# Two hybrid decoder layers on one core: new prices and a new limit in the estimate that orders the mixing stage

## The chip, the cores and the metric
The kernel runs on one core of a Trainium2 chip. The metric is the time of one execution on the device in microseconds (us). TensorE does the matrix products (PE in the profile), VectorE (DVE), ScalarE (ACT) and GpSimd (POOL) the rest, and SyncE (SP) starts the DMA transfers.

## What is computed
Input and output are 512 tokens of 1024 channels in float32. Two layers of the same form follow each other:

```python
for l in range(DEPTH):                       # DEPTH = 2
    x = _layernorm(ALPHA * x + 0.5 * _swiglu(x, ffn1_w_in[l], ffn1_w_out[l]), ...)
    mix = _hybrid_mixer(x, l, mix_w_in[l], ...)
    x = _layernorm(ALPHA * x + mix, ...)
    x = _layernorm(ALPHA * x + 0.5 * _swiglu(x, ffn2_w_in[l], ffn2_w_out[l]), ...)

def _hybrid_mixer(x, ...):
    h = x @ w_in                             # one projection for everything below
    ya = _rwkv7(h[..., 0:o1], ...)           # 8 heads of 64: decay, delta rule, group norm
    yb = _diff_attention(h[..., o1:o2], ...) # 4 heads: two softmaxes, one minus lam times the other
    yc = _gated_deltanet(h[..., o2:o3], ...) # 4 heads: causal conv, chunks of 64, gated delta rule
    branches = jnp.einsum('blnc,ncd->blnd', stack([ya, yb, yc]), w_branch)
    gates = sigmoid(h[..., o3:])
    return (gates * branches summed over the three) @ w_out
```

## The kernel before, in words
**Products.** The stream is held transposed as two parts of float32r, a high part `xTh` and a low part `xTl`; a weight tile `wr` comes by DMA, ScalarE casts its high part `wh`, VectorE subtracts to get the low part `wl`, and a product is made of three matmuls, high by high, low by high and high by low, each 128x512. A column of the projection is 8 tiles of 128 channels, so 24 such matmuls (`proj`, tile name `pj`; `pz` and `pgt` are the same for other columns). They depend on nothing but the weights and the stream, so TensorE can do them at any time: they are what fills it between the mixers' small products.

**The mixing stage.** It has 12 units, in the order `R D R D R R D G G D G G` (`ORDER`), numbered from 0 within their kind: R is a pair of RWKV heads (`rw_pair`), D a head of differential attention (`da_head`), G a head of the gated delta rule (`gdn_head`). For each unit the projection columns are made first (3 or 4), then the unit's mixer starts as a generator that does one step, yields, does the next. `gdn_ab` and its chain of small VectorE operations (tiles `gq`, `gg`, then the products `pG`) come after R0. At the end `merge` multiplies the three branches by their gates; for each branch it first has every open mixer of that kind run out (`finish`).

**What sets the order.** Everything is issued in the order in which the Python program calls it, and a framework's scheduler may then move instructions a little on each engine. `interleave` alternates: one step of the main generator (a few products), then as many steps of open mixers as `pump` gives, until the estimated time of TensorE has grown by `CAP` = 1300 ns. `Estimate` (L81 to L131) keeps that time: `log` adds to each engine's clock the price of an instruction (`c_pe`, `c_act`, two lambdas), and notes when each tile will be ready. A mixer's next step is taken when the estimated end of its last step (`it[2]`) is no later than TensorE's estimated clock (`self.est.pe.t`). A price that is too low makes a step look ready too early, so that it is issued with too little other work ahead of it.

**The limit on open units.** Before a new unit may have its columns made, `unit` (L1334) calls `pump(True)` while four mixers are open. A forced pump takes the mixer whose last step ends first by the estimate, ready or not. The tiles of the mixers come from one pool of 53 buffers of 128x512 (`T2B`).

**Names used below.** R unit: `pM` are the chunk products that VectorE masks into `M`; `pMV`, `paT` are turned into `R` by VectorE; `pW` is the product of the solved triangle `iZ` by `R`; then a scan of four steps `pU`, `VU`, `pS`, `S`; `Y` is the group-normed result, `pyT<-Y` its transposes, `pgl` its gate. D unit: `pdo` the attention's output, `dO` its scaling by the norm (`norm_T`), `pyT<-dO` its transposes. G unit: `pk`, `gL`, `gr` the decays, `iZ`, `ip` the solving of the triangle, `pv`, `vn`, `po`, `gO` the scan, `pyT<-gO` the transposes; `cv`, `ct` the convolution in `gdn_conv`. `rst`, `rsy` are the tiny operations of a reciprocal square root on VectorE (`rsqrt`), `Tb` and `LX` those that solve a triangle by rows.

Of the kernel before, what the change touches and what calls it, by code (L numbers as in the profile page):

```python
# [13 lines left out]
ALU = mybir.AluOpType  # L14
# [29 lines left out]
AHEAD = 2  # L44
LOADED = 1
BLK = 8 * (16 * 128 + 16)
WIDTH = 4
CAP = 1300.0
PJB = 3
T2B = 53  # L50
# [4 lines left out]
class Queue:  # L55


    def __init__(self, eng, cost, est):
        self.eng, self.cost, self.est, self.t = eng, cost, est, 0.0
        self.last, self.inorder = None, False  # L60
# [20 lines left out]
class Estimate:  # L81
# [3 lines left out]
    def __init__(self, tc):  # L85
        nc = tc.nc
        self.tc = tc
        q = lambda eng, cost: Queue(eng, cost, self)
        self.nc, self.ready, self.stage = nc, {}, 0.0
        self.tensor = q(nc.tensor, self.c_pe)  # L90
        self.vector = q(nc.vector, lambda op, n, k: 70 + n * (0.52 if op in ("tensor_scalar", "tensor_copy") else 1.04))
        self.scalar = q(nc.scalar, self.c_act)
        self.gpsimd = q(nc.gpsimd, lambda op, n, k: 600 + 150 * n if k.get("op") == ALU.pow else 150 + 2.1 * n)
        self.sync = q(nc.sync, None)
        self.pe = self.tensor
        self.queues = (self.tensor, self.vector, self.scalar, self.gpsimd)
# [8 lines left out]
    def c_pe(self, op, n, k):  # L105
        m = k["out"].shape[0]
        if op == "transpose":
            return 107
        if k["rhs"].dtype == F32R:
            return n / 2.4 / (1 if m > 32 else 4)  # L110
        return max(107, n / 0.6) / (1 if m > 64 else 1.7 if m > 32 else 2.7)

    def c_act(self, op, n, k):
        return 80 + n / 1.2 + (94 if any(hasattr(k.get(x), "tensor") for x in ("scale", "bias")) else 0)

    def log(self, q, op, args, kw):
        names = ("out", "lhsT", "rhs") if op == "matmul" else ("out", "in_", "identity")
# [17 lines left out]
class Net:  # L135
# [1196 lines left out]


    def unit(self, n, h):  # L1334
        while sum(it[0] < 3 for it in self.active) >= WIDTH:
            self.pump(True)
        cols = (h, 4 + h, 8 + h)
        if n == 0:
            mixer, cols = self.rw_pair, [self.rw_col(c) for c in cols]
        elif n == 1:  # L1340
            mixer, cols = self.da_head, [self.da_col(c) for c in cols]
        else:
            mixer, cols = self.gdn_head, [self.gdn_conv(c) for c in (4 + h, h, 8 + h)] + [self.gdn_z()]
        f = []
        for g in cols:
            f.append((yield from g))
            yield
        self.active.append([n, mixer(h, *f), self.est.stage])
# [73 lines left out]
```

## Time and profile before

| what | value |
|---|---|
| median of 3 runs | 2872.88 us (2869.75 to 2876.25) |
| the profiled execution's own time | 2870.58 us |
| its span, first to last instruction | 2868.8 us |
| mean granted clock of TensorE | 0.998 |
| PE busy | 2819.2 us, 98% of the span |
| DVE busy | 1651.9 us, 58% |
| ACT, POOL busy | 1009.7 us, 158.3 us |
| mixing stage of the first layer | about 400 to 900 us of the span |
| mixing stage of the second layer | about 1827 to 2327 us |

In the timeline views a row has start, duration, engine, line, operation, output and inputs, shape and count, and in brackets the idle time just before it on its engine with what ended it. Matmuls overlap in the records (one of 128x512 is listed at 0.39 us and the next begins about 0.23 us later), so idle time below some 0.16 us before a matmul is not seen. Almost every instruction is put down to one line (L66), the recording helper; tiles' names tell them apart.

### The profile page before, as it was taken

How to read it: one execution, taken by the hardware profiler on the slowest of the kernel's cores; microseconds unless marked ns; L12 is line 12 of the kernel's file. 1: busy time of each engine (PE TensorE's matmuls, PEld its weight loads, DVE VectorE, ACT ScalarE, POOL GpSimd, SP SyncE). 2: the span in 40 equal slices, each digit the busy share in tenths (PEclk: the TensorE clock that was granted, in tenths of full speed). 3: DMA queues.
4: the chain of work that ended last, by engine and by line, in shares of the span. 5: the costliest groups of instructions: out<-in, count | busy, mean ns of one | idle time of the engine just before them, and what ended most of it. 6: DMA issues, size and time to landing. Idle time of an engine off the chain costs nothing. (4 is left out here: it accounts for less than half of the span.)

```text
span 2868.8 us, 40154 instructions
## 1 busy us (share of the span) xinstructions
PE 2819.2 (98%) x15728; PEld 2331.8 (81%) x15728; DVE 1651.9 (58%) x3752; ACT 1009.7 (35%) x1797; POOL 158.3 (6%) x204
## 2 busy tenths in 40 slices
PE   9999999999999999999999999999999999999998
PEld 8888887778888888888888888777788888888887
DVE  4333567788874463433643445677888755633345
ACT  3222345444543332222322223454545433322222
POOL 1000021110000010000100000211100000100001
PEclk9999999999999999999999999999999999999999
DMA  6433423222232353333424334232221334533332
GB/s 179 127 100 97 142 78 81 70 62 61 61 83 82 96 177 103 104 101 97 147 89 126 96 96 139 84 81 58 69 61 53 86 86 116 163 109 97 96 96 88
DMA packets 436349, 282.17 MB, mean 98 GB/s; under 512 B 39432, under 2 KB 391872, under 8 KB 436160
## 3 DMA queue, kind: packets, MB, share of 16 engines
q1 hardware_dynamic: 436160, 279.60, 33.4%
q8 instruction: 124, 2.03, 0.3%
q14 instruction: 65, 0.53, 0.1%
HBM read 258.31 MB, written 21.25 MB: 97 GB/s over the span
## 5 line engine op out<-in xcount | busy, mean ns | idle before, releaser
L66 DVE TENSOR_TENSOR wl<-wr,wh 128x1024 fp32r<-128x1024 f32 x406 | 502.1, 1237 | 648.9 <-ACT wh L66 647.8
L66 ACT CAST wh<-wr 128x1024 fp32r<-128x1024 f32 x406 | 427.5, 1053 | 1229.8 <-issue 535.8
L66 PE MATMUL pu<-xTh,wh 128*128 128x512 f32 x672 | 261.6, 389 | 0.0
L66 PE MATMUL pu<-xTl,wh 128*128 128x512 f32 x672 | 261.5, 389 | 0.0
L66 PE MATMUL pu<-xTh,wl 128*128 128x512 f32 x672 | 261.4, 389 | 0.0
L66 PE MATMUL oa<-wh,hl 128*128 128x512 f32 x640 | 249.0, 389 | 0.0
L66 PE MATMUL pg<-xTl,wh 128*128 128x512 f32 x640 | 249.0, 389 | 0.0
L66 PE MATMUL oa<-wh,hh 128*128 128x512 f32 x640 | 249.0, 389 | 0.0
L66 PE MATMUL pg<-xTh,wh 128*128 128x512 f32 x640 | 249.0, 389 | 0.0
L66 PE MATMUL pg<-xTh,wl 128*128 128x512 f32 x640 | 249.0, 389 | 0.0
L66 PE MATMUL oa<-wl,hh 128*128 128x512 f32 x640 | 249.0, 389 | 0.0
L66 PE MATMUL pj<-xTh,wh 128*128 128x512 f32 x560 | 228.5, 408 | 1.5 <-DVE sh L66 1.5
L66 PE MATMUL pj<-xTl,wh 128*128 128x512 f32 x560 | 225.0, 402 | 0.0
L66 PE MATMUL pj<-xTh,wl 128*128 128x512 f32 x560 | 223.9, 400 | 0.0
L66 DVE TENSOR_TENSOR ft<-ft,pu 128x512 f32<-128x512 f32 x84 | 57.8, 688 | 226.9 <-PE pu L66 226.8
L66 PE MATMUL pgt<-xTh,wh 128*128 128x512 f32 x384 | 154.1, 401 | 0.0
L66 PE MATMUL pgt<-xTh,wl 128*128 128x512 f32 x384 | 150.5, 392 | 0.0
L66 PE MATMUL pgt<-xTl,wh 128*128 128x512 f32 x384 | 149.6, 390 | 0.0
L66 PEld LDWEIGHTS pu<-xTh,wh 128*128 128x128 f32 x672 | 126.3, 188 | 26.1
L66 PEld LDWEIGHTS pu<-xTh,wl 128*128 128x128 f32 x672 | 126.1, 188 | 26.1
L66 PEld LDWEIGHTS pu<-xTl,wh 128*128 128x128 f32 x672 | 126.2, 188 | 26.0
L66 PEld LDWEIGHTS pg<-xTl,wh 128*128 128x128 f32 x640 | 120.2, 188 | 25.1
(392 smaller groups left out, 5282.5 us busy)
## 6 DMA issues: line engine op xcount, KB each, us to landing
wr<-in_ffn_w_in_dram SPq DMA_DIRECT2D x176, 512.0 KB
wr<-in_mix_w_in_dram SPq DMA_DIRECT2D x132, 512.0 KB
wr<-in_ffn_w_out_dram SPq DMA_DIRECT2D x88, 512.0 KB
wr<-in_mix_w_branch_dram SPq DMA_DIRECT2D x24, 512.0 KB
xres<-x SPq DMA_DIRECT2D x40, 256.0 KB
x<-xres SPq DMA_DIRECT2D x40, 256.0 KB
wr<-in_mix_w_out_dram SPq DMA_DIRECT2D x16, 512.0 KB
iX<-Xd SPq DMA_DIRECT2D x24, 256.0 KB
```

Source lines behind the costliest of these rows:

```text
L66: r = f(*args, **kw)
```

## The change
The estimate gets other prices on all engines, and the limit on open units another measure. `WIDTH` becomes 17 and is held against a sum of `ROOM`, 5 for an open R unit, 4 for a D, 4 for a G, 0 for the scalars' entry, with the new unit's own room included. VectorE costs 145 + 1.06 ns per element for every operation (62 more where a scalar comes from a tile); before it was 70 + 0.52 for `tensor_scalar` and `tensor_copy` and 70 + 1.04 for the others. ScalarE's base goes from 80 to 165, with 190 more for a sum on the side; GpSimd's from 150 to 250; float32r matmuls get 13.3 ns more and lose the division for few rows; float32 matmuls go from n / 0.6 to n / 0.57.

```diff
-WIDTH = 4
+WIDTH = 17
+ROOM = (5, 4, 4, 0)
...
-        self.vector = q(nc.vector, lambda op, n, k: 70 + n * (0.52 if op in ("tensor_scalar", "tensor_copy") else 1.04))
+        self.vector = q(nc.vector, self.c_dve)
         self.scalar = q(nc.scalar, self.c_act)
-        self.gpsimd = q(nc.gpsimd, lambda op, n, k: 600 + 150 * n if k.get("op") == ALU.pow else 150 + 2.1 * n)
+        self.gpsimd = q(nc.gpsimd, lambda op, n, k: 600 + 150 * n if k.get("op") == ALU.pow else 250 + 2.1 * n)
...
         if k["rhs"].dtype == F32R:
-            return n / 2.4 / (1 if m > 32 else 4)
-        return max(107, n / 0.6) / (1 if m > 64 else 1.7 if m > 32 else 2.7)
+            return n / 2.4 + 13.3
+        return max(112, n / 0.57) / (1 if m > 64 else 1.7 if m > 32 else 2.7)
 
     def c_act(self, op, n, k):
-        return 80 + n / 1.2 + (94 if any(hasattr(k.get(x), "tensor") for x in ("scale", "bias")) else 0)
+        return 165 + n / 1.2 + (94 if any(hasattr(k.get(x), "tensor") for x in ("scale", "bias")) else 0) + \
+            (190 if k.get("accum_out") is not None else 0)
+
+    def c_dve(self, op, n, k):
+        return 145 + 1.06 * n + (62 if any(hasattr(k.get(x), "tensor") for x in ("scalar", "scalar1")) else 0)
...
     def unit(self, n, h):
-        while sum(it[0] < 3 for it in self.active) >= WIDTH:
+        while sum(ROOM[it[0]] for it in self.active) + ROOM[n] > WIDTH:
             self.pump(True)
```

The limit bites at other units. Before, `pump` was forced ahead of the columns of R2 (three times), R3 (32), G1, G2 and G3. With the room, it is forced ahead of D1 (R0, D0 and R1 are open, and 14 + 4 is over 17), R2, D2, G0 (R2, R3 and D2 are open, again 14 + 4; 40 times, until D2 has ended), G1 and G3.

No instruction is added or taken away: TensorE, VectorE and the others have the same ones, in the feed-forward stages in the same order; in the mixing stages of both layers they stand in another order, the same in both. Since one line is added near the top, the helper's line is L67 in the kernel after. Three places of the new order follow; a row has the operation, output and inputs, the output's shape and the count.

**The solve of R1, on TensorE.** Before, this stands where unit R1's triangle is solved (`pW` is the product that needs the solved triangle) while unit D0 and the pair R0 end:

```order
L66 MATMUL paT<-ident,AR 128x128
L66 MATMUL pyT<-ident,dO 128x128 x2
L66 MATMUL paT<-ident,AR 128x128 x2
L66 MATMUL pW<-iZ,R 64x128 x8
L66 MATMUL pU_4777<-R,iZ 64x64 x16
L66 MATMUL pyT<-ident,Y 128x128 x4
L66 MATMUL pgl<-gdh,gup 128x512
L66 MATMUL pgl<-gdl,gup 128x512
L66 MATMUL pgl<-gdh,gup 128x512
L66 MATMUL pS<-VU,KB 128x128
L66 MATMUL pU<-M,R 128x128
L66 MATMUL pj<-xTh,wh 128x512
```

In the change the same place on TensorE reads:

```order
L67 MATMUL pyT<-ident,Y 128x128 x4
L67 MATMUL pgl<-gdh,gup 128x512
L67 MATMUL pgl<-gdl,gup 128x512
L67 MATMUL pgl<-gdh,gup 128x512
L67 MATMUL paT<-ident,AR 128x128 x4
L67 MATMUL pj<-xTh,wl 128x512
L67 MATMUL pj<-xTh,wh 128x512
L67 MATMUL pj<-xTl,wh 128x512
L67 MATMUL pj<-xTh,wl 128x512
L67 MATMUL pj<-xTh,wh 128x512
L67 MATMUL pW<-iZ,R 64x128 x8
L67 MATMUL pU_4532<-R,iZ 64x64 x16
```

Before, no product of the projection stands between `paT` and the scan's second step; now five stand between `paT` and `pW`, and nine more follow before the scan's `pS`. The transposes of `dO` have gone elsewhere.

**The start of R3, on TensorE and VectorE.** This is where unit R3's `pM` products end, while R2's scan (`pU`, `pS`) and unit D2's norm (`dss`, `dO`) run. In the change TensorE has, after the last `pM`:

```order
L67 MATMUL pS<-VU,KB 128x128
L67 MATMUL pj<-xTl,wh 128x512
L67 MATMUL pj<-xTh,wl 128x512
L67 MATMUL pyT<-ident,dO 128x128
L67 MATMUL pU<-M,R 128x128
L67 MATMUL pyT<-ident,dO 128x128 x3
L67 MATMUL pMV<-VU,M 64x64 x16
L67 MATMUL pS<-VU,KB 128x128
L67 MATMUL pU<-S,R 128x128
L67 MATMUL paT<-ident,AR 128x128 x4
L67 MATMUL pW<-iZ,R 64x128 x8
L67 MATMUL pU_5862<-R,iZ 64x64 x16
```

and VectorE at the same place, from the third of R3's four masks `M<-pM`:

```order
L67 TENSOR_TENSOR M<-pM,m_372 128x384
L67 SCALAR_TENSOR_TENSOR rst<-rst,dss 128x4
L67 TENSOR_TENSOR M<-pM,m_372 128x384
L67 SCALAR_TENSOR_TENSOR rsy<-rst,rsy 128x4
L67 TENSOR_TENSOR M<-pS,M 128x128
L67 TENSOR_TENSOR rst<-rsy 128x4
L67 SCALAR_TENSOR_TENSOR M<-M,Ef,bd 128x128
L67 SCALAR_TENSOR_TENSOR rst<-rst,dss 128x4
L67 TENSOR_TENSOR wl<-wr,wh 128x1024
L67 SCALAR_TENSOR_TENSOR dss<-rst,rsy 128x4
L67 TENSOR_SCALAR dO<-dO,dss 128x128 x4
L67 TENSOR_TENSOR VU<-pU,R 64x128
```

Before, 17 products of the projection stood between R3's `paT` and `pW`; now two stand from the last `pM` to the end of the solve. `pU`, `pS`, `VU` and `S` in between are R2's scan.

**The end of G0's scan, on VectorE.** In the change VectorE has, from the last `vn` of the scan (it needs `pv`) on, with the convolution of the next unit's column (`cv`) and the solving of another unit's triangle (`Tb`, `LX`) between:

```order
L67 COPY vn<-pv 128x128
L67 TENSOR_TENSOR iZ<-iZ,ip 128x512
L67 STREAM_TRANSPOSE iX<-iZ 128x512
L67 TENSOR_TENSOR gO<-gO,po 128x128
L67 TENSOR_SCALAR iZ<-ip 32x4x32 x2
L67 SCALAR_TENSOR_TENSOR cv<-pj,pt,cv 128x511
L67 TENSOR_SCALAR gss<-gss 128x4
L67 TENSOR_TENSOR Tb<-LX 32x15
L67 SCALAR_TENSOR_TENSOR cv<-pj,pt,cv 128x510
L67 TENSOR_SCALAR rst<-gss 128x4
L67 TENSOR_TENSOR LX<-LX,Tb 32x15
L67 SCALAR_TENSOR_TENSOR cv<-pj,pt,cv 128x509
```

24 more instructions follow, 22 of them tiny, one `rv` and one `ct`, and then `gO<-gO,gss` x4, which `pyT<-gO` on TensorE needs. TensorE has from that `pv` to `pyT<-gO` six small products of 128x128 (`ip`, `po`), 20 of 32x32 and 14 of `pz`.

## Rows read from the trace of the kernel before

**Rows 1.** The page's totals for TensorE (busy time, share of the span, instructions) and the clock granted to it in 40 equal slices, in tenths.
```profile
PE 2819.2 (98%) x15728; PEld 2331.8 (81%) x15728; DVE 1651.9 (58%) x3752; ACT 1009.7 (35%) x1797; POOL 158.3 (6%) x204
PEclk9999999999999999999999999999999999999999
```

**Rows 2.** Stretches of the span: a feed-forward stretch, then the early and the late part of each layer's mixing stage. Columns: length, busy time (and count) of PE, PEld, DVE, ACT, POOL, granted clock, share of the DMA engines, GB/s.
```profile
100.00:200.00 100.00, 100.00 (x443) 82.84 (x442) 38.84 (x44) 25.84 (x31) 0.00 (x0) 1.00 0.33 99
400.00:574.00 174.00, 163.61 (x1233) 129.91 (x1232) 133.40 (x433) 87.01 (x180) 24.06 (x28) 0.99 0.30 76
574.00:900.00 326.00, 322.33 (x2319) 262.44 (x2318) 258.44 (x874) 149.56 (x366) 17.04 (x25) 1.00 0.25 67
1827.00:2001.00 174.00, 162.85 (x1235) 128.79 (x1234) 134.20 (x432) 86.81 (x179) 23.06 (x28) 1.00 0.30 76
2001.00:2327.00 326.00, 322.12 (x2319) 262.29 (x2318) 258.51 (x874) 149.57 (x366) 16.84 (x24) 1.00 0.25 67
```

**Rows 3.** What TensorE waited for from 400 to 574 us: total, times, longest. Only the larger rows that are not in the next group.
```profile
PE pG L66 <- DVE gg L66: 2.0, 1, 2.0
PE pyT L66 <- DVE dO L66: 1.8, 2, 1.3
PE ip L66 <- DVE iZ L66: 1.1, 2, 0.9
PE pb L66 <- DVE dmx L66: 1.1, 1, 1.1
```

**Rows 4.** TensorE in order of time, where R1's `pM` end and its triangle is solved.
```profile
549.90 0.32 PE L66 MATMUL pM<-AR,sh 64*64 64x128 f32 x1
...
550.73 1.16 PE L66 MATMUL pdo<-dv,dsc 128*128 128x128 f32 x8
...
555.48 0.33 PE L66 MATMUL pMV<-VU,M 64*64 64x64 f32 x4 [0.75 <-DVE M L66]
...
560.41 0.30 PE L66 MATMUL pyT<-ident,dO 128*128 128x128 f32 x1 [0.49 <-DVE dO L66]
...
562.87 1.09 PE L66 MATMUL pW<-iZ,R 128*64 128x128 f32 x16 [1.40 <-DVE Tb L66]
563.77 1.13 PE L66 MATMUL pU<-R,iZ 128*64 128x64 f32 x32
564.83 0.66 PE L66 MATMUL pyT<-ident,Y 128*128 128x128 f32 x4
...
566.67 0.49 PE L66 MATMUL pS<-VU,KB 128*128 128x128 f32 x2 [0.48 <-ACT VU L66]
567.60 0.49 PE L66 MATMUL pU<-M,R 128*128 128x128 f32 x2 [0.44 <-DVE M L66]
568.86 0.63 PE L66 MATMUL pj<-xTh,wh 128*128 128x512 f32 x1 [0.77 <-DVE sh L66]
```

**Rows 5.** VectorE at the same place, in order of time. Between the first and the last row of the tiny operations stand 21 others of their kind.
```profile
557.63 0.16 DVE L66 TENSOR_TENSOR rst<-rsy 128x8 f32<-128x8 f32 x1
...
559.32 0.14 DVE L66 SCALAR_TENSOR_TENSOR dss<-rst,rsy 128x4 f32<-128x4 f32 x1
559.40 0.67 DVE L66 TENSOR_TENSOR Y<-Y,gn 128x512 f32<-128x512 f32 x1
560.00 0.85 DVE L66 TENSOR_SCALAR dO<-dO,dss 128x128 f32<-128x128 f32 x4
560.78 0.21 DVE L66 TENSOR_TENSOR LX<-LX,Tb 64x64 f32<-64x64 f32 x1
560.92 1.20 DVE L66 TENSOR_TENSOR wl<-wr,wh 128x1024 fp32r<-128x1024 f32 x1
562.05 0.67 DVE L66 TENSOR_TENSOR R<-paT,nn 128x512 f32<-128x512 f32 x1
```

**Rows 6.** VectorE's groups from 400 to 900 us, shapes kept apart: count, then busy us and mean ns of one, then the idle time before.
```profile
L66 DVE SCALAR_TENSOR_TENSOR cv<-pj,pt,cv 128x511 f32<-128x511 f32 x12 | 8.9, 739 | 0.8 <-ACT cv L66 0.7
L66 DVE STREAM_TRANSPOSE iX<-iZ 128x512 f32<-128x512 f32 x12 | 8.4, 702 | 0.1
L66 DVE TENSOR_TENSOR M<-pM,m 128x384 f32<-128x384 f32 x16 | 8.2, 546 | 0.1
L66 DVE SCALAR_TENSOR_TENSOR ct<-ct,cv 128x512 f32<-128x512 f32 x12 | 8.2, 683 | 1.2 <-ACT ct L66 1.2
L66 DVE TENSOR_TENSOR VU<-pU,R 64x128 f32<-64x128 f32 x28 | 8.0, 285 | 7.0 <-PE pU L66 6.5
L66 DVE TENSOR_SCALAR iZ<-ip 32x128 f32<-32x128 f32 x24 | 6.8, 283 | 3.8 <-PE ip L66 3.2
L66 DVE SCALAR_TENSOR_TENSOR M<-M,Ef,bd 128x128 f32<-128x128 f32 x12 | 4.2, 352 | 0.1
L66 DVE TENSOR_SCALAR dO<-dO,dss 128x128 f32<-128x128 f32 x16 | 3.5, 278 | 0.0
L66 DVE TENSOR_TENSOR R<-pMV,nn 128x512 f32<-128x512 f32 x4 | 2.8, 689 | 1.3 <-PE pMV L66 1.2
L66 DVE TENSOR_SCALAR lw<-lw 128x512 f32<-128x512 f32 x4 | 1.7, 426 | 1.1 <-ACT lw L66 1.1
```

**Rows 7.** TensorE's granted clock right after that place, in the first layer and in the second; columns as in the second group.
```profile
568.00:572.00 4.00, 3.23 (x10) 2.56 (x10) 2.61 (x7) 0.00 (x0) 0.00 (x0) 0.63 0.45 131
1996.00:2000.00 4.00, 3.33 (x16) 2.54 (x16) 2.68 (x6) 0.00 (x0) 0.00 (x0) 1.00 0.45 131
```

## The prediction
> **What bounds the kernel now.** I read the totals first: TensorE is busy for 98% of the span, every other engine for 58% or less [rows 1]. So the end is set by TensorE's own work plus the time in which it stands, and a change that leaves the work alone can only move the standing time. Next I read the windows, to see where it stands. A feed-forward stretch has none (100.00 of 100, 443 matmuls, so 100 / 443 = 0.226 us from one 128x512 matmul to the next) [rows 2]. The mixing stage has 174 - 163.61 = 10.4 us in its early part and 326 - 322.33 = 3.7 in its late part, in the second layer 11.2 and 3.9: 29.1 us in the two layers [rows 2]. VectorE is at 133.4 of 174 = 77% in the early part, 79% in the late: loaded, not full [rows 2]. So TensorE stands at places where small products that need VectorE follow each other with no projection product between.
>
> Then the waits: in the early part `pG` waits 2.0 us for the end of a VectorE chain, `pyT` 1.3 and 0.5 for `dO`, `ip` 1.1, `pb` 1.1 [rows 3]. The timeline shows the rest in one place, the solve of R1: 0.75, 0.49, 1.40, 0.48, 0.44 and 0.77, together 4.33 us within 14 [rows 4]. VectorE's timeline says why: with two reciprocal roots and a triangle on it, 23 tiny operations take 1.7 us, then come `Y`, four `dO` and a weight split `wl` of 1.20 us before the `R` that `pW` needs [rows 5].
>
> **What is left alone.** The change adds and removes no instruction, so the busy time of TensorE stays at its 2819.2 us [rows 1], and so do the feed-forward stages. The new prices are never executed; they cost nothing themselves. Transfers: the order of weight tiles is that of the plan, and the matmuls waiting for none of them in these windows is how I take the DMA queue to be no part of it (0 us; the DMA engines are at 25 to 33% [rows 2]).
>
> **R1's solve: -4.0 us per layer.** In the new order five projection products stand between `paT` and `pW` (5 x 0.226 = 1.1 us) and nine before the first `pS` (2.0 us), and `dO` with its transposes is gone from there. The 1.40 of `pW` came from `Y`, `dO` and `wl` ahead of `R`; the products now ahead of `pW` and after it cover what is left. I keep 0.3 for a `pS` behind `VU` and take 4.33 - 0.3 = 4.0 off. Bounds: -2.5 (only the three long waits 1.40 + 0.49 + 0.77 go) to -4.33.
>
> **R3's start: +5.3 us per layer.** The dense place is not gone, it comes back here. After the last `pM` TensorE has one `pS` and two products before it needs `dO`: 0.25 + 0.45 = 0.7 us. VectorE has from the third mask on: two `M` (0.546 each), `M<-pS` (about a `VU`'s 0.285), a scaled `M` (0.352), `wl` (1.20), five tiny ones at some 0.08 [rows 5, 6] and then the first `dO`. Operations overlap by some 0.06 each in the timeline, so this is 1.03 + 0.23 + 0.29 + 1.13 + 0.4 = 3.1 us, plus one `dO` and the way to TensorE, 0.3. That alone is 3.4 - 0.7 = 2.7 of waiting; TensorE makes the sixteen products of a pair of masks in 0.4 us (four masks' worth lasts 550.73 - 549.90 = 0.8 [rows 4]) while VectorE takes 1.03 for a pair, so VectorE is about another 0.5 behind when the last `pM` ends. I take 3.2. Then three more chains have almost no cover: the next `dO`s 0.2; the scan's `pU` behind `VU`, `R<-pMV` (0.689), `S` and its scaling, against 1.2 us of `pyT`, `pMV` and `pS`, 1.1; `pW` behind another `VU` and `R<-paT` (0.67 [rows 5]), against `pU` and `paT`, 0.8. Sum 3.2 + 0.2 + 1.1 + 0.8 = 5.3. Before, 17 products (3.8 us) stood between `paT` and `pW` here and nothing of this showed. Bounds: 1.0 (VectorE runs ahead of TensorE here, and only `wl` shows) to 7.
>
> On the four `dO`: the timeline has 0.85 us for four, 278 ns as a mean of one [rows 5, 6]. [...]
>
> **The end of G0's scan: +2.5 us per layer.** From the last `vn` on VectorE has `vn` (like `dO`, 0.28), `iZ<-iZ,ip` (like `ct`, 0.68), the transpose (0.70), `gO` (0.28), two `iZ<-ip` (0.57), three `cv` (2.2), `ct` (0.68), `rv` (0.28), some 25 tiny ones (1.7 to 2.3 at the pace of [rows 5]) and the first `gO` again (0.28): 7.7 to 8.3, less overlap (12 x 0.06 = 0.7), 7.0 to 7.6 [rows 6]. TensorE has 14 products (3.2 us), six small ones (about 0.8, by the pace of the `pyT` rows, 0.66 for four) and 20 tiny ones (about 1.3: `pU` runs 32 instructions in 1.06 [rows 4]): 5.3. Difference 1.7 to 2.3, plus the way over two queues: 2.5. Bounds: 0 (VectorE is ahead of TensorE when `pv` comes, and the convolution already done) to 4.
>
> **pG: +0.6 us per layer.** The chain of small operations that ends in `gg` now shares VectorE with three `wl`, eight `L` and more; I put the 2.0 [rows 3] at 2.6. Bounds: 0 (all hidden) to 4, so -2.0 to +2.0.
>
> **The rest.** The other early waits (`ip`, `pb`, the first `dO`, 1.1 + 1.1 + 1.3 [rows 3]) I leave, between -1.5 and +1.5, because units D1 and R2 are held back by forced pumps there. The 3.7 us of small waits in the late part [rows 2] should shrink with the better prices of short VectorE and ScalarE operations (base 145 in place of 70): I take -1.0, between -2 and +1.
>
> **The clock: +0.8 us in all.** [...] It cost (1 - 0.63) x 4 = 1.5 us once. The place at R3 stands longer in both layers; I give it a fall and a half against one: +0.8, between -1.5 and +1.7.
>
> **Sum.** Per layer -4.0 + 5.3 + 2.5 + 0.6 - 1.0 = +3.4; twice, +6.8; with the clock +7.6. The profiled execution took 2870.6 us, so 2878.2; the median of the runs stands 2.3 above it, which gives 2880.5, and I say **2880**.
>
> **Rivals.** A measurement of this kernel tells about 0.2%, 5.7 us, from no change.
>
> 1. *The new dense places are covered* (faster). R1's waits go, the tiny operations of D2's norm are done before R3's masks, so R3 costs 1.0 and G0 nothing; late waits lose 2. Per layer -4.0 + 1.0 + 0.6 - 2.0 = -4.4, and the fall of the clock goes: -8.8 - 1.5 = -10.3, 2863. For it: prices of 145 ns and more are nearer to the rows (285 for 64x128 where the old price gives 70 + 1.04 x 128 = 203), and steps should be issued less early. Against it: the two products behind the last `pM`.
>
> 2. *The waits only change places* (no change). R3 3.0, G0 1.0: -4.0 + 3.0 + 1.0 + 0.6 - 1.0 = -0.4 per layer, 2872. For it: VectorE has the same load, and its 77 to 79% [rows 2] leaves about the same slack anywhere.
>
> 3. *Forced pumps starve TensorE* (much slower). With the room, D1, R2, D2 and G0 wait for a unit to end; where nothing else is open, products for filling are only those that the three buffers of `pj` allow. The price is half of the early part's idle time again, 5 us per layer on top of the forecast, and one more fall: 7.6 + 10 + 1.7 = 19.3, 2892. It decides if the early part's VectorE share goes above some 82% while TensorE's falls.
>
> That the change does nothing is excluded: the order differs from R0 on.
>
> **Chances.** The forecast 0.42, rival 1 0.28, rival 2 0.20, rival 3 0.10. The forecast's own range is 2874 to 2886, of which a small part lies within 0.2%: faster 0.28, same 0.24, slower 0.48. The range takes in rival 1 but for its lower half, and reaches to rival 3: 2861 to 2892.
>
> **What would show it.** Right: at R1's solve `pW` follows without idle time, and `pyT<-dO` after the `pM` of R3 has some 3 us before it, `pU` and `pW` after it about 1 each; `pyT<-gO` of G0 has 2 to 3. TensorE's busy time in the mixing stage stays, its idle time goes from 29 to about 36. Wrong: if the waits of [rows 4] are still there, or if R3's transposes find `dO` ready; if idle time in the late part grows, the prices made it worse where I expect them to help.

## The result and the profile after
The change takes **2914.85 us** (median of 4 runs, 2913.31 to 2916.58) against 2874.18 for the kernel before beside it: ratio **1.0148**, 95% interval 1.0133 to 1.0163. It is slower, as forecast, but by 41 us and not by 7; 2880 is far off and 2892, the end of the range, too low.

The profiled execution has a span of 2911.8 us, 43.0 longer. The page's totals and clock of the change, which answer to [rows 1]:

```profile
PE 2836.7 (97%) x15728; PEld 2346.5 (81%) x15728; DVE 1668.1 (57%) x3752; ACT 1010.7 (35%) x1797; POOL 170.4 (6%) x204
PEclk9999999999999999999999999999999999999999
```

TensorE is busy for 17.5 us more with the same 15728 instructions, and stands for 43.0 - 17.5 = 25.5 us more. The windows over the mixing stages of the change (the late part 22 us longer, the second layer 22 us later; columns as in [rows 2]):

```profile
400.00:574.00 174.00, 168.46 (x1290) 131.63 (x1289) 134.54 (x418) 85.96 (x178) 20.52 (x26) 0.99 0.28 72
574.00:922.00 348.00, 326.19 (x2243) 268.14 (x2242) 260.86 (x856) 147.23 (x353) 24.70 (x26) 0.95 0.25 66
1849.00:2023.00 174.00, 168.65 (x1292) 131.68 (x1291) 134.29 (x417) 85.85 (x177) 22.33 (x26) 0.99 0.28 72
2023.00:2371.00 348.00, 325.88 (x2250) 267.77 (x2249) 261.57 (x859) 147.69 (x355) 25.41 (x26) 0.96 0.25 66
```

The early part has become better: 174 - 168.46 = 5.5 us of standing, where [rows 2] had 10.4. The late part has 21.8 where there were 3.7. So the added standing is all in the later half, where VectorE's share has gone down, 75% after 79%. What TensorE waited for, over the whole run of the change (total, times, longest):

```profile
PE pj L67 <- DVE dk L67: 10.1, 2, 5.0
PE pk L67 <- POOL sh L67: 7.4, 2, 3.7
PE pG L67 <- DVE gg L67: 6.2, 2, 3.1
PE pyT L67 <- DVE dO L67: 5.8, 2, 2.9
PE pz L67 <- DVE rsy L67: 5.5, 2, 2.8
...
PE pd L67 <- DVE gr L67: 3.1, 4, 1.2
PE pk L67 <- DVE gL L67: 3.1, 2, 1.6
```

The first two were in no list of mine. The `pk` stands early in unit R3, well before its `pM`, and waits for GpSimd. Timelines of TensorE, GpSimd and VectorE there, in the change:

```profile
589.27 0.40 PE L67 MATMUL pj<-xTh,wl 128*128 128x512 f32 x1
593.37 1.12 PE L67 MATMUL pk<-ident,sh 128*128 128x128 f32 x4 [3.70 <-POOL sh L67]
...
586.03 2.50 POOL L67 TENSOR_TENSOR AR<-sh,lw 128x256 f32<-128x256 f32 x2
588.49 2.50 POOL L67 TENSOR_TENSOR imL<-L,lev 128x512 f32<-128x512 f32 x2
590.94 2.37 POOL L67 TENSOR_TENSOR sh<-sh,G 128x512 f32<-128x512 f32 x1
...
587.26 0.67 DVE L67 TENSOR_TENSOR y<-y,sh 128x512 f32<-128x512 f32 x1
587.86 0.74 DVE L67 TENSOR_TENSOR Tb<-LX 64x64 f32<-64x64 f32 x1
...
592.12 1.27 DVE L67 TENSOR_TENSOR LX<-LX,Tb 64x63 f32<-64x63 f32 x1
...
593.58 0.20 DVE L67 TENSOR_TENSOR Tb<-LX 64x60 f32<-64x60 f32 x1
```

R3's `sh` stands behind two products `imL` of another unit's triangle in GpSimd's queue, and takes 2.37 us itself, where each of the four in a layer took 1.27 to 1.29 before. VectorE's tiny operations are listed at 0.74 and 1.27 us there, at 0.20 as soon as GpSimd's products have ended (593.3 us). So a part of the 3.70 us is that the two engines slow each other (in e7 below a tiny operation of VectorE comes every 1.22 us in place of every 0.25). Then the projection itself waits, for the eviction of a column (timelines of TensorE, ScalarE and VectorE in the change):

```profile
607.00 0.39 PE L67 MATMUL pj<-xTh,wl 128*128 128x512 f32 x1
612.43 0.76 PE L67 MATMUL pj<-xTh,wh 128*128 128x512 f32 x1 [5.05 <-DVE dk L67]
...
607.20 1.04 ACT L67 CAST wh<-wr 128x1024 fp32r<-128x1024 f32 x1 [4.38 <-PE pj L67]
608.26 1.17 ACT L67 CAST dk<-pj 64x512 fp32r<-64x512 f32 x2
...
608.27 1.22 DVE L67 TENSOR_TENSOR wl<-wr,wh 128x1024 fp32r<-128x1024 f32 x1 [0.24 <-ACT wh L67]
609.52 0.68 DVE L67 TENSOR_TENSOR dk<-pj,dk 64x512 fp32r<-64x512 f32 x1
...
611.59 0.69 DVE L67 TENSOR_TENSOR dk<-pj,dk 64x512 fp32r<-64x512 f32 x1
```

This is a ring. TensorE's last product of a column frees a weight buffer at 607.2; ScalarE, which stood 4.38 us for it, casts `wh`; behind that cast in ScalarE's queue stand the casts of `dk` that empty an older column (D2's keys, whose last product ran some 27 us before the wait ended), and VectorE's share of `dk` follows them; and the next column needs the buffer of that older one, the third of three. No engine is overloaded; each waits for another. The `wl` on VectorE adds little: it ends at 609.49, and ScalarE's first two casts of `dk` end at 609.43. [rows 4] had a hint of it: its `pj` stood 0.77 us for `sh`, which is an eviction too.

The granted clock right after such waits (columns as in [rows 2]; [rows 7] had one such window in two layers):

```profile
596.00:600.00 4.00, 4.00 (x11) 3.08 (x11) 3.80 (x7) 0.59 (x1) 1.78 (x2) 0.53 0.41 116
612.00:616.00 4.00, 3.57 (x12) 2.61 (x12) 2.75 (x10) 2.62 (x6) 0.00 (x0) 0.50 0.40 114
664.00:668.00 4.00, 3.47 (x48) 3.50 (x48) 2.54 (x4) 0.65 (x2) 0.00 (x0) 0.57 0.01 4
796.00:800.00 4.00, 4.00 (x21) 4.00 (x21) 0.68 (x2) 1.20 (x3) 1.27 (x1) 0.50 0.71 197
```

Over the mixing stages of the change the windows of 4 us lie between 0.50 and 1.00, called the lower and the upper level here; at 0.50, products of 128x512 follow each other 0.43 us apart (five intervals from 597.12 to 599.25 us). In the first window TensorE is busy all the time and gets through 11 matmuls; at the pace of [rows 2] it would be 4 / 0.226 = 18. Over the mixing stages, in windows of 4 us, (1 - clock) x 4 adds up to 34 us in the change and to 1.7 before.

### The profile page after: what moved, and what is told of

It reads as the page before. It is cut to its first block, busy times and chain, and to the rows that moved or that the text cites. A ratio compares the mean times of both kernels' runs of the same rounds, so it can differ in the third digit from the quotient of the medians.

```text
span 2911.8 us, 40172 instructions
## 1 busy us (share of the span) xinstructions
PE 2836.7 (97%) x15728; PEld 2346.5 (81%) x15728; DVE 1668.1 (57%) x3752; ACT 1010.7 (35%) x1797; POOL 170.4 (6%) x204
## 5 line engine op out<-in xcount | busy, mean ns | idle before, releaser
L67 DVE TENSOR_TENSOR wl<-wr,wh 128x1024 fp32r<-128x1024 f32 x406 | 500.1, 1232 | 658.8 <-ACT wh L67 658.0
L67 ACT CAST wh<-wr 128x1024 fp32r<-128x1024 f32 x406 | 427.2, 1052 | 1230.9 <-issue 556.2
L67 PE MATMUL pu<-xTh,wh 128*128 128x512 f32 x672 | 261.6, 389 | 0.0
L67 PE MATMUL pu<-xTh,wl 128*128 128x512 f32 x672 | 261.4, 389 | 0.0
L67 PE MATMUL pu<-xTl,wh 128*128 128x512 f32 x672 | 261.4, 389 | 0.0
L67 PE MATMUL oa<-wh,hl 128*128 128x512 f32 x640 | 249.0, 389 | 0.0
L67 PE MATMUL pg<-xTh,wh 128*128 128x512 f32 x640 | 249.0, 389 | 0.0
L67 PE MATMUL pg<-xTl,wh 128*128 128x512 f32 x640 | 249.0, 389 | 0.0
L67 PE MATMUL pg<-xTh,wl 128*128 128x512 f32 x640 | 249.0, 389 | 0.0
L67 PE MATMUL oa<-wh,hh 128*128 128x512 f32 x640 | 249.0, 389 | 0.0
L67 PE MATMUL oa<-wl,hh 128*128 128x512 f32 x640 | 249.0, 389 | 0.0
L67 PE MATMUL pj<-xTh,wh 128*128 128x512 f32 x560 | 228.6, 408 | 11.2 <-DVE dk L67 10.1
L67 PE MATMUL pj<-xTl,wh 128*128 128x512 f32 x560 | 227.6, 406 | 0.0
L67 PE MATMUL pj<-xTh,wl 128*128 128x512 f32 x560 | 225.1, 402 | 0.0
L67 DVE TENSOR_TENSOR ft<-ft,pu 128x512 f32<-128x512 f32 x84 | 57.7, 687 | 227.5 <-PE pu L67 227.4
L67 PE MATMUL pgt<-xTh,wh 128*128 128x512 f32 x384 | 154.6, 403 | 0.0
L67 PE MATMUL pgt<-xTh,wl 128*128 128x512 f32 x384 | 150.4, 392 | 0.0
L67 PE MATMUL pgt<-xTl,wh 128*128 128x512 f32 x384 | 150.1, 391 | 0.0
L67 PEld LDWEIGHTS pu<-xTl,wh 128*128 128x128 f32 x672 | 126.2, 188 | 26.1
L67 PEld LDWEIGHTS pu<-xTh,wh 128*128 128x128 f32 x672 | 126.2, 188 | 26.1
L67 PEld LDWEIGHTS pu<-xTh,wl 128*128 128x128 f32 x672 | 126.0, 188 | 26.1
L67 PEld LDWEIGHTS pg<-xTh,wl 128*128 128x128 f32 x640 | 120.3, 188 | 24.9
```

Of the source, the lines that this page charges most:

```text
L67: r = f(*args, **kw)
```

## The experiments
All times are medians beside runs of the kernel before (2873 to 2874 us). Two theories stood at first: **L**, the new limit makes the loss; **P**, the new prices do.

**e1_prices: the new prices, the old limit.**
```diff
-WIDTH = 17
-ROOM = (5, 4, 4, 0)
+WIDTH = 4
-        while sum(ROOM[it[0]] for it in self.active) + ROOM[n] > WIDTH:
+        while sum(it[0] < 3 for it in self.active) >= WIDTH:
```


> The new prices with the old limit of four open units. Theory L (the limit: with 17 for R, D and G only three units fit beside an R, so pumps are forced ahead of D1, R2, D2 and G0 and TensorE runs small products without projection products between): the loss is gone, 2862 to 2880 us, no wait of 3 us or more at pk, pj or pz, and one or two falls of the clock. Theory P (the prices: steps are issued later, columns of the projection are spent early, and evictions and chains pile up on VectorE): the loss stays, 2900 to 2920 us, with the same waits pk <- sh of 3.7 and pj <- dk of 5.


Measured: 2855.83 us, ratio 0.9935 (0.9920 to 0.9951). The prices are a gain of 17 us, more than theory L asked for. It is the fastest kernel of the study.

**e2_room: the new limit, the old prices.**
```diff
-WIDTH = 4
+WIDTH = 17
+ROOM = (5, 4, 4, 0)
-        while sum(it[0] < 3 for it in self.active) >= WIDTH:
+        while sum(ROOM[it[0]] for it in self.active) + ROOM[n] > WIDTH:
```


> The new limit (17, room 5, 4, 4) with the old prices. Theory L: most of the loss is here, 2895 to 2920 us, with a wait of some 3 to 5 us ahead of the products of D2 or G0. Theory P: about the time of the kernel before, 2865 to 2882.


Measured: 2890.40, ratio 1.0056 (1.0041 to 1.0071). The sign is theory L's; the +17 us are below its range, and the wait of 3 to 5 us that it named isn't there (the longest in the first layer is 2.01, at a `pyT`). The parts don't add: -17 and +17 alone, +41 together; under the new prices the limit costs 2915 - 2856 = 59 us.

**e3_w18 and e4_w19: 18 or 19 in place of 17** (e4 with 19 in the last line).
```diff
-WIDTH = 17
+WIDTH = 18
```


> The change with 18 in place of 17: two R, a D and another D or G fit together, so the pumps ahead of D1 and G0 go; those ahead of R2 and D2 (19) stay. Theory L: about half of the 42 us is gone, 2885 to 2900. Theory P: within 6 us of the change, 2908 to 2920.


Measured: 2878.39, ratio 1.0015 (1.0006 to 1.0025).


> The change with 19 in place of 17: R, R, D and R fit too, so none of the pumps ahead of D1, R2, D2 and G0 need be forced for the fourth unit. Theory L: as the new prices with the old limit, 2862 to 2880. Theory P: within 6 us of the change, 2908 to 2920.


Measured: 2871.73, ratio 0.9994 (0.9984 to 1.0003). Theory P is out: with the new prices in place, the limit alone takes the loss away. 18 takes away 36 of the 41 us, better than expected; it lets a fourth unit open ahead of D1 and of G0. 19 still holds R3 back where the old limit doesn't, and takes 16 us more than e1.

**e5_pjb4: the change with a fourth buffer for the projection's columns** (the ring above).
```diff
-PJB = 3
+PJB = 4
```


> The change with four buffers in place of three for the projection's columns (and four in place of five for the other accumulators). In the change a column waits 5.05 us for the eviction dk of a column that ended 27 us before. Theory B (the buffer is what it waits for, because the evictions of D2's columns stand late in VectorE's queue): that wait goes in both layers with the fall of the clock behind it, about 2 x (5.05 + 2) = 14 us, so 2898 to 2906 us. Theory S (TensorE runs dry here whatever the buffers, the wait turns up at the next small product): within 4 us of the change, 2911 to 2919; slower if the small products miss the fifth buffer.


Measured: 2897.80, ratio 1.0090 (1.0073 to 1.0107): 17 us less than the change. The row of that `pj`:
```profile
608.36 0.50 PE L67 MATMUL pj<-xTh,wh 128*128 128x512 f32 x1 [1.18 <-DVE dk L67]
```
5.05 has become 1.18. Theory B holds for the wait: the buffer is what the column waited for. Of the 17 us, 2 x (5.05 - 1.18) = 7.7 are this wait; the order of the matmuls moves with the buffer too, and other waits with it (`pk` from 3.70 to 2.58). That leaves 24 us over the kernel before.

**e6_kap: the product `sh` of the R unit on VectorE, priced as on GpSimd.**
```diff
-        nc.gpsimd.tensor_tensor(out=kap, in0=k, in1=G, op=ALU.mult)
+        kw = dict(out=kap, in0=k, in1=G, op=ALU.mult)
+        i = nc.vector.eng.tensor_tensor(**kw)
+        self.est.log(nc.gpsimd, "tensor_tensor", (), kw)
+        nc.vector.order(i.ins)
```


> The change with the product of k and G (tile sh, 128x512) of the R unit on VectorE instead of GpSimd, the estimate still pricing it on GpSimd. In the change pk waits 3.70 us for it behind two imL on GpSimd. Theory G (GpSimd's queue is what pk waits for): 3.7 and part of a fall of the clock go in each layer, 8 to 12 us less, 2902 to 2908 us. Theory V (VectorE is the one that is late there, and has one operation of 0.68 more now): pk waits for VectorE instead, within 4 us of the change, 2911 to 2919.


Measured: 2911.21, ratio 1.0134 (1.0119 to 1.0149), 4 us less than the change, within the two intervals.
```profile
598.21 0.50 PE L67 MATMUL pj<-xTh,wh 128*128 128x512 f32 x1 [3.31 <-DVE dq L67]
...
610.74 0.77 PE L67 MATMUL pj<-xTh,wh 128*128 128x512 f32 x1 [5.19 <-DVE dk L67]
```
The wait of `pk` is gone and a `pj` waits 3.31 us for VectorE a few us later. So theory G is right on the wait and wrong on the time. The time is theory V's, but what waits is a column for its buffer (`dq` is D2's queries), not `pk`: the next thing is late.

**e7_micro: VectorE's chains alone and beside GpSimd.** The layers are left out; chains (`d...A` alone, `d...P` beside six GpSimd products of 128x512) in which each operation needs the one before:
```python
V.tensor_tensor(out=t[0:64, 0:63], in0=t[0:64, 0:63], in1=x1[0:64, 0:63], op=ALU.mult)   # tiny
V.tensor_tensor(out=t, in0=t, in1=x1, op=ALU.mult)                                       # big
V.tensor_tensor(out=t[:, 0:128], in0=pp[:, 0:128], in1=t[:, 0:128], op=ALU.mult)         # psum: pp in PSUM
V.tensor_scalar(out=t[:, 0:128], in0=t[:, 0:128], scalar1=0.5, scalar2=None, op0=ALU.mult)  # scal
```


> Only a measurement: chains of dependent VectorE operations, first alone, then beside six 128x512 products of two tiles on GpSimd; the layers are left out and the output is zeros. In the change the tiny operations Tb and LX are listed at 0.69 to 1.93 us while GpSimd multiplies and at 0.2 when it doesn't. Theory H (the two engines hold each other up): tiny products 64x63 rise from 0.2 to 0.5 us or more beside GpSimd, and GpSimd's from 1.2 to 2 us or more. Theory W (the long rows are waits that the record counts as work): 0.2 in both. What the products with an operand in PSUM and the tensor_scalar do tells whether it is both operands in SBUF that matters.


Measured, groups by line and shape (busy us, mean ns):
```profile
L44 DVE TENSOR_TENSOR dbigP<-dbigP,x 128x512 f32<-128x512 f32 x12 | 12.1, 1005 | 0.4
L48 DVE TENSOR_SCALAR dscalP<-dscalP 128x128 f32<-128x128 f32 x24 | 11.2, 466 | 0.8
L42 DVE TENSOR_TENSOR dtinyP<-dtinyP,x 64x63 f32<-64x63 f32 x24 | 11.0, 457 | 0.8
L44 DVE TENSOR_TENSOR dbigA<-dbigA,x 128x512 f32<-128x512 f32 x12 | 8.3, 692 | 0.4
L48 DVE TENSOR_SCALAR dscalA<-dscalA 128x128 f32<-128x128 f32 x24 | 5.4, 227 | 0.8
L42 DVE TENSOR_TENSOR dtinyA<-dtinyA,x 64x63 f32<-64x63 f32 x24 | 5.2, 216 | 0.8
L46 DVE TENSOR_TENSOR dpsumA<-pp,dpsumA 128x128 f32<-128x128 f32 x16 | 4.7, 291 | 0.5
L46 DVE TENSOR_TENSOR dpsumP<-pp,dpsumP 128x128 f32<-128x128 f32 x16 | 4.7, 291 | 0.5
```
and VectorE's timeline, where GpSimd's six products run from 12.38 to 19.98 us:
```profile
12.79 7.26 DVE L42 TENSOR_TENSOR dtinyP<-dtinyP,x 64x63 f32<-64x63 f32 x6
...
20.08 0.97 DVE L42 TENSOR_TENSOR dtinyP<-dtinyP,x 64x63 f32<-64x63 f32 x4
...
80.53 7.27 DVE L48 TENSOR_SCALAR dscalP<-dscalP 128x128 f32<-128x128 f32 x6
```
The groups marked P mix both: only the first operations of each chain run beside GpSimd. The first six tiny products took 7.29 us up to the start of the seventh, the next four, after GpSimd's last product, 0.97. That is 1.22 against 0.25 each: one tiny product for each of GpSimd's, which follow each other 1.22 us apart. With one operand in PSUM nothing changes, 291 and 291 ns. Theory H holds for VectorE; GpSimd's products stayed at 1.26 us beside the tiny ones, against H, and rose to 1.70 beside the big ones. What couples the two engines is not shown.

**e8_p_dve and e9_p_rest: half of the prices, the old limit** (VectorE's new ones alone; all but VectorE's).
```diff
-        self.vector = q(nc.vector, self.c_dve)
+        self.vector = q(nc.vector, lambda op, n, k: 70 + n * (0.52 if op in ("tensor_scalar", "tensor_copy") else 1.04))
```


> The old limit of four units, with only VectorE's new prices; those of ScalarE, GpSimd and TensorE are the old ones. The new prices together gave -17.6 us. Theory V (VectorE is what TensorE waits for, so its prices make the gain): 2852 to 2862 us. Theory O (the other engines' prices, ScalarE's base of 165 above all, since most steps end in a ScalarE copy): 2866 to 2878.


Measured: 2883.02, ratio 1.0034 (1.0021 to 1.0047).


> The old limit of four units, the new prices of ScalarE, GpSimd and TensorE and the old ones of VectorE: the other half of the split. All new prices gave -17.6 us, VectorE's alone +9.9. Theory A (each price has a worth of its own, and they add): -27, 2842 to 2851 us. Theory N (they don't add: the estimate decides by differences between engines' clocks, and half a set of prices sets these wrong too): nearer to the kernel before than to the full set, 2862 to 2890.


Measured: 2866.82, ratio 0.9975 (0.9964 to 0.9985). The diff is e9's; e8 is the other way round. +10 and -6 make +4, both together make -17. Neither V nor A; e8 is above O's range too. The prices have no worth of their own that adds up, and the range of N holds.

**e10_prices_pjb4: e1 with four buffers.**
```diff
-PJB = 3
+PJB = 4
```


> All new prices, the old limit of four units, and four buffers for the projection's columns. With the limit of 17 the fourth buffer gave -17 us. Theory B (it helps where columns' evictions are late, which is at the forced pumps of 17): TensorE waits at no column with the limit of four, so within 6 us of 2856, 2850 to 2862. Theory F (a fourth buffer lets more projection products stand ready everywhere): 2840 to 2849. A loss, 2863 and more, would say that the small products need the fifth buffer that is taken from them.


Measured: 2858.09, ratio 0.9945 (0.9929 to 0.9961), as theory B says: with four units open the fourth buffer takes nothing off the time.

**e11_d1 and e12_g0: one of the two forced stretches** (e12 with (2, 0) in the last line).
```diff
-WIDTH = 17
+WIDTH = 18
-        while sum(ROOM[it[0]] for it in self.active) + ROOM[n] > WIDTH:
+        while sum(ROOM[it[0]] for it in self.active) + ROOM[n] > WIDTH - ((n, h) == (1, 1)):
```


> The change with 18 everywhere but 17 ahead of D1: of the two stretches that 17 forces and 18 doesn't, only the one ahead of D1 (27 pumps). 18 took 2878, 17 took 2915: 36.5 us. Theory D (the early stretch does it: it puts R1 and R2 and D2's columns late, and with them the waits of 3.70 at pk and 5.05 at pj): 2895 to 2910. Theory G (the stretch ahead of G0 does it, with R3's start and the waits at pd, pk and pz after it): 2875 to 2888.


Measured: 2914.75, ratio 1.0144 (1.0128 to 1.0160).


> The change with 18 everywhere but 17 ahead of G0 (40 pumps). Theory D: 2875 to 2888. Theory G: 2895 to 2910. If both this and the run with D1 alone lie near 2878, the loss is made by the two together; if both lie above 2890 they add.


Measured: 2919.36, ratio 1.0159 (1.0143 to 1.0175). Each costs the whole, and both together cost no more. The case of sums that I had named ("both above 2890, they add") is wrong as well: 36 and 41 do not make 36. In e12 the waits of 3.70 and 5.05 aren't there; others are (4.81 and 4.04 at `ip`).

**e13_w15, e14_w15_col, e15_prices_col: a stricter limit (e13, the first two lines alone), and the pumps behind a unit's first column (e14, the whole).**
```diff
-WIDTH = 17
+WIDTH = 15
...
-        while sum(ROOM[it[0]] for it in self.active) + ROOM[n] > WIDTH:
-            self.pump(True)
-        for g in cols:
+        for i, g in enumerate(cols):
+            if i == 1:
+                while sum(ROOM[it[0]] for it in self.active) + ROOM[n] > WIDTH:
+                    self.pump(True)
```


> The change with 15 in place of 17: at most three units, two when an R and two D or G are open is still three, and no fourth at all. Theory T (with three units open TensorE has too little ready work while a pump is forced; the stricter, the worse): 2915 to 2945 us. Theory K (17 loses by the particular order it happens to give, not by the number of open units): anywhere from 2870 to 2910.


Measured: 2919.38, ratio 1.0160 (1.0145 to 1.0175).


> The same limit of 15, but the forced pumps of a unit come after its first column of the projection and not ahead of it, so 24 products of 128x512 (5.4 us of TensorE's time) lie ready beside each forced stretch. Theory T: the lack of projection products in the forced stretch is what costs, so 15 to 40 us less than with 15 ahead of the columns. Theory K: another order, a change of either sign, within 10 us.


Measured: 2912.34, ratio 1.0138 (1.0121 to 1.0155).


> The new prices with the old limit of four units (2856 us), the forced pumps again after the first column of a unit. Theory T: with four units open TensorE is short of work in few places (13 us of waits in each layer), so a gain of 0 to 8 us, 2848 to 2856. Theory K: within 10 us either way.


This is e1 with its loop moved in the same way. Measured: 2867.90, ratio 0.9978 (0.9969 to 0.9988). It is above T's range and just outside K's.

e13 lies in T's range, but it is hardly a stricter test. 15 differs from 17 only where at most one of four units would be an R, first ahead of D3, so TensorE's order is the change's own up to 710 us of the span. In e14 the gain of 7 us is K's size and not T's. But e14 does not put projection products between the forced steps: the column goes ahead of them, and the steps still follow each other. TensorE then stands at the first product of two columns, again for the eviction of the column three back, whose last `cv` ended just before (timeline of TensorE, first layer; `rst` is a tiny operation beside that `cv`):
```profile
708.28 0.77 PE L67 MATMUL pj<-xTh,wh 128*128 128x512 f32 x1 [5.44 <-DVE rst L67]
...
782.55 0.77 PE L67 MATMUL pj<-xTh,wh 128*128 128x512 f32 x1 [3.80 <-DVE cv L67]
```
So a lack of projection products in the forced stretch, theory T's explanation, is neither shown nor ruled out. A column ahead of the pumps gives 7 us with the strict limit and takes 12 with the old one.

## Why the prediction was wrong
The sign was right. The mechanism that I made the likeliest, waits that move, was given +7 of the 41 us. Rival 3, forced pumps, named the limit, with a chance of 0.10 and half of the price, but not the place: in the early part VectorE's share stayed at 77% and TensorE's rose to 97%, and the loss is in the late part. By my own sign, growing idle time there would have meant that the prices made it worse; e1 shows the opposite, they take 17 us off.

Term by term, in the first layer, idle time of TensorE before and after (us):

| term | forecast | measured |
|---|---|---|
| R1's solve | -4.0 | -3.8 (0.38 and 0.17 are left) |
| R3's start | +5.3 | +5.5 |
| around G0's scan's end | +2.5 | +6.5 |
| `pG` | +0.6 | +1.05 |
| other early waits | 0 | -2.1 |
| `pk` behind GpSimd, `pj` behind the ring | none | +8.75 |
| late small waits | -1.0 | -2.6 |
| sum | +3.4 | +13.3 |

**R1 and R3** came out as worked out from the order and the durations, R3's sum in part by luck. The rows of R3's start in the change:

```profile
654.05 0.49 PE L67 MATMUL pS<-VU,KB 128*128 128x128 f32 x2 [0.74 <-DVE VU L67]
657.87 0.45 PE L67 MATMUL pyT<-ident,dO 128*128 128x128 f32 x1 [2.88 <-DVE dO L67]
662.73 0.49 PE L67 MATMUL pU<-S,R 128*128 128x128 f32 x2 [1.03 <-DVE S L67]
664.53 1.96 PE L67 MATMUL pW<-iZ,R 128*64 128x128 f32 x16 [0.88 <-DVE R L67]
```

2.88, 1.03 and 0.88, where I had 3.2, 1.1 and 0.8; the 0.74 at `pS` I did not have. One reading was off: the 0.8 us of `pM` in [rows 4] are 32 products, two masks and not four, so VectorE falls some 0.3 behind there and not 0.5. The four `dO` took 0.88 us in the change, as the row had it.

**G0's scan** did not come out. I had not looked at the products ahead of it, which wait for the decays; and the 2.77 us at the first of the 14 `pz` have the size that I gave to `pyT<-gO` by luck (timelines of TensorE and, for `cv`, VectorE):

```profile
792.35 0.39 PE L67 MATMUL pd<-gr,r_le 128*128 128x256 f32 x1 [1.18 <-DVE gr L67]
...
795.31 1.22 PE L67 MATMUL pk<-ct 128*128 128x128 f32 x4 [1.55 <-DVE gL L67]
...
806.88 0.76 PE L67 MATMUL pz<-xTh,wh 128*128 128x512 f32 x1 [2.77 <-DVE rsy L67]
...
812.24 0.38 PE L67 MATMUL pyT<-ident,gO 128*128 128x128 f32 x2
...
806.00 0.73 DVE L67 SCALAR_TENSOR_TENSOR cv<-pj,pt,cv 128x509 f32<-128x509 f32 x1
```

`pyT<-gO` has no idle time before it. `pz` opens a column, and no `pz` reads `rsy`, a tiny operation that ended 0.08 us behind this `cv`. The `cv` is the last that empties the column three back, whose products ended at 770 us: the same kind of wait as in the ring.

**The step that failed first is what "The rest" says of the late part**, -1.0 us per layer with bounds of -2 to +1. Its small waits did shrink, but 8.75 us of `pk` and `pj` stand there, for which no term was given, and 2.77 of `pz`, which I had put to another cause. The forecast rested on walking VectorE's queue against TensorE's at the places that looked dense. GpSimd's queue, where `sh` stands behind `imL`, was not walked at all, though it was in the order, and neither was the question which column's eviction frees the buffer of the next one, and what stands ahead of it: on ScalarE a `wh` that waits for TensorE, on VectorE steps of a solve that wait for TensorE. The forecast had also taken every projection product as ready at any time, as the description of the kernel does; the first product of a column needs a free accumulator (only rival 3 named the three buffers). e5 shows that this term counts: with a fourth buffer 17 us go. The traces show it too. In every run of the two layers, TensorE's idle time ahead of `pj`, `pz` and `pgt` in the mixing stages stands at the first product of a column. In both layers together it is 16.8 us in the change, 25.2 in e6 and 9.0 to 19.3 in e11 to e14; it is 1.5 in the kernel before, 5.1 in e1, and at most 6.2 in all other runs.

**The second is the clock**, +0.8 forecast, worked out from one fall, the 0.63 of [rows 7] over 4 us; summed in the same way, the mixing stages of the change have 34 us. The waits themselves make 25.5 of the 43.0 us; the 17.5 us of longer busy time are more than the forecast's whole sum. Of these some 9 come from 128x512 products that follow each other at the lower level (50 such intervals, 10.5 us longer than at the upper, against 6 and 1.3 before). The rest is not taken apart: TensorE stood at the lower level for 68 us of the two mixing stages, busy for 59 of them, against 3.4 before, and what the small products lose there is not told from what the new order gives or takes. In the first layer of the change the clock fell behind `pG` (3.06), `pk` (3.70), `pj` (5.05), R3's start (5.5 in 11 us) and the two waits at 792 to 807 us; so its cost goes with the waits, and I should have given it to each of the places that I forecast.

**The third is the sum's premise**, that the busy time stays and only visible idle time can move. e1 is 17 us faster than the kernel before, with idle time of TensorE 48.1 us against 49.6 and less busy time for the same instructions. Its page answers to [rows 1]:

```profile
PE 2804.1 (98%) x15728; PEld 2332.0 (82%) x15728; DVE 1654.6 (58%) x3752; ACT 1009.5 (35%) x1797; POOL 158.3 (6%) x204
```

From the first layer's first projection product to 1000 us TensorE goes 153 times in e1 from products of the projection and the merge (`pj`, `pz`, `pgt`, `pbr`) to small ones, before 165 times. The intervals at these changes, there and back, come to 53.2 us, before 60.5; those between small products to 164.6, before 167.8 (idle time left out). So in e1 the time fell in intervals that no list of waits has. Whether they hold waits too short to be listed is not shown. The change has 165 such turns again.

On what the limit does, under the new prices: 17 gives 2915, 15 gives 2919, D1 or G0 alone 2915 and 2919, a column ahead 2912; with the fourth unit let in at both places the runs lie between 2856 and 2878. So a fourth unit held back at one of two places makes some 40 us, at both no more. Forced pumps as such are not it: counted in one layer, as the kernels issue their steps, there are 112 in e1, 143 in e3, 142 in e11 and 161 in the change, 90 in the kernel before and in e15. The time from the first projection product of the first layer's mixing stage to the first one of `merge` (`pgt`) tells the two sorts apart: 397 us in e1, e3 and e4, 393 in e15, 401 before; 422 in the change, 417 to 425 in e11 to e14. It does not for e5, which has 401 and loses its time behind that point. What the kernels from 2911 to 2919 us share is late evictions of columns, and more time at the lower clock: 51 to 82 us in the two mixing stages, against 17 to 21 in e1, e3, e4 and e15. Why holding back a fourth unit at one place is enough for that **stays open**: the waits are at different places in e11 and e12, and no run here tests a lack of projection products cleanly.

## What to carry to other kernels
Where a planner's limit or prices reorder a program, walk every queue at each new neighbourhood, GpSimd's and that of the buffers too: for each buffer that changes hands, the accumulators of independent products too, ask which instruction frees it and what stands ahead of that one in its queue. Test the parts of such a change alone and together, as they need not add, and expect scatter from the order alone: e8, e9 and e15 moved the time by 6 to 12 us either way. Here a wait behind which TensorE's clock fell cost its own length and the slower products behind it, 0.43 us from one 128x512 product to the next in place of 0.226.

## What the runs showed of the hardware
Beside GpSimd's products of two 128x512 tiles, VectorE's tiny operations with both operands in SBUF came every 1.22 us in place of every 0.25, one for each GpSimd product. A `tensor_scalar` of 128x128 was held up likewise (six in 7.27 us, 227 ns each alone), and a `tensor_tensor` of 128x512 took 1.63 us in place of 0.69, with GpSimd's own at 1.70 in place of 1.26 (e7). With an operand in PSUM there was nothing of it (291 ns alone and beside GpSimd). In the change, in such a stretch of 7 us (586 to 593), `sh` took 2.37 us in place of 1.27 to 1.29, and the steps of VectorE's solve 0.69 to 1.27 in place of 0.20. That it made D2's evictions late is not shown: VectorE stood idle for 2.25 us after it, ahead of the `wl` at 602.84, waiting for ScalarE's `wh`.
